# The two merge gates of a hybrid encoder's mixer: sixteen plain products per layer rewritten as eight pairs of seven block products

## The chip, the cores and the metric

The kernel runs on one core of one Trainium2 chip. The metric is the device time of that core in microseconds (us). The median of three runs of the kernel before is 1674.38 us (1673.81 to 1674.62). The core's engines are TensorE (PE, with its weight load listed apart as PEld), VectorE (DVE), ScalarE (ACT), GpSimd (POOL) and SyncE (SP), which issues most of the DMAs.

## What is computed

Two layers of an encoder on a sequence of 512 rows of width 1024, in float32. Each layer is a mixer (attention and a short convolution side by side, merged by two sigmoid gates) and a SwiGLU feed-forward part (FFN). Cut to what matters:

```python
for l in range(DEPTH):                       # DEPTH = 2
    h = rms_norm(x, g_pre_mix[l])
    q, k, v, cb, cc, cx, ga, gb = jnp.split(h @ w_in[l], splits, axis=-1)
    ...
    y_attn = band_attention(q, k, v, attn_sink[l]) @ w_attn_proj[l]
    y_conv = (cb * short_conv(cc * cx, conv_w[l])) @ w_conv_proj[l]
    mix = (jax.nn.sigmoid(ga) * y_attn + jax.nn.sigmoid(gb) * y_conv) @ w_out[l]
    x = x + rms_norm(mix, g_post_mix[l])
    h = rms_norm(x, g_pre_ffn[l])
    f = (jax.nn.silu(h @ w_gate[l]) * (h @ w_up[l])) @ w_down[l]
    x = x + rms_norm(f, g_post_ffn[l])
```

`ga` and `gb` are 1024 columns each of the input projection `h @ w_in`.

## The kernel before

**Precision.** Every float32 operand is held as a high part (rounded to the format that TensorE takes) and a low part (the rest), and every product is three matmuls: high by low, low by high, high by high (`mm3`, L175 to L177). Splitting a weight tile is one ACT copy that rounds (L130) and one DVE subtraction (L131), for a tile of 128 partitions by 512 elements; splitting an activation is the same pair on L206 and L207.

**Plain products.** `gemm` computes 128 output columns for all 512 rows of the sequence: 8 steps along the width, 3 matmuls each, 24 matmuls of 512 moving columns. Its weights come by one DMA of 512 KB into one of three `raw` tiles and are split into two of eight `hl` tiles.

**Seven block products.** The FFN's gate and up products are done in pairs (`class Pair`): for one block f, 128 columns of w_gate and 128 of w_up are the two rows of a 2 by 2 block matrix whose columns are the two halves of the width, and the activations are a 2 by 2 block matrix too (halves of the width by halves of the sequence). Seven products of sums of blocks replace the eight plain ones. Each product is 4 steps of 3 matmuls with 256 moving columns. `Pair.prep` adds weight blocks on DVE (L393) and splits each sum (L130, L131); `Pair.product` runs the matmuls and takes the results out of the banks with small ACT and DVE instructions (L434 to L448). Loads of the second matrix go into tiles of the pool `u4` (22 buffers). `orders` writes down in which order the products of several pairs follow each other, and weights are prepared `AHEAD = 5` products early. The sums of the activations' blocks (`Rights`) are made once per layer.

**The stage of the change.** After the attention and the convolution's projection (`conv_proj`), a loop over m = 0 to 7 runs three plain products: the columns `GB0 + m` of w_in, a sigmoid (L783) and a multiplication by the convolution's branch (L785); the columns `GA0 + m` and their sigmoid (L788); the attention's projection, a multiplication (L791), an addition (L792) and a split into `mix[m]`. Then `down` multiplies by w_out: rows k = 0 to 2 stream through `hl` tiles for all eight output banks, rows 3 to 7 are split into ten `u4` tiles and kept, and the last part runs row block by row block (t = 0 to 3), so that the normalisation of block t (`post_norm`, L257 to L264; `pre_norm`, L236) goes on beside the products of block t + 1. In between stand the loads and splits of the first FFN weights (`ahead`).

**Order.** A scheduler puts each engine's instructions into one fixed order when the program is built; each engine then runs its own list strictly in that order and waits where an operand or a buffer isn't there. The rows under the change below show these lists.

## Time and profile before

| | |
|---|---|
| median of three runs | 1674.38 us |
| the profiled execution: its time, its span | 1674.66 us, 1672.9 us |
| busy: PE, PEld, DVE, ACT, POOL | 1650.1, 1454.9, 1141.8, 862.7, 72.3 us |
| first layer: loop over m, from its first matmul to the first of `down` | 314.35 to 444.90 us |
| second layer: the same | 1141.06 to 1271.62 us |

Busy time is the sum of an engine's instruction spans; overlapping spans count once. A row of the timeline gives the start, the duration, the engine, the line and the operation, and in square brackets for how long the engine had been idle and what released it. Matmuls overlap in the pipeline, so their pace is read from the distance between starts.

### The profile page before, as it was taken

The page shows a single profiled execution, that of the slowest core. Times are in us where ns is not written, and L with a number is a line of the kernel's source. Part 1 is how long each engine was busy: PE and PEld are TensorE (multiplying, and loading weights), DVE is VectorE, ACT ScalarE, POOL GpSimd, SP SyncE. Part 2 cuts the span into 40 slices and gives each one's busy share as a digit, 9 for nine tenths or more (in the row PEclk, how much of TensorE's full clock was granted, in tenths as well). Part 3 has the DMA queues.
Part 4 walks back from the last instruction along what each step waited for, and adds up shares of the span by engine and source line. Part 5 has one row for each costly group of instructions (what it writes and reads, how often), then busy time and mean ns, then how long its engine had stood idle before and what let it go on. Part 6 is the DMA issues. An engine that isn't in the chain of part 4 may idle for free.

```text
span 1672.9 us, 24896 instructions
## 1 busy us (share of the span) xinstructions
PE 1650.1 (99%) x9457; PEld 1454.9 (87%) x9457; DVE 1141.8 (68%) x2230; ACT 862.7 (52%) x1806; POOL 72.3 (4%) x114
## 2 busy tenths in 40 slices
PE   7999999999999999999999999999999999999998
PEld 7888888888889999988898888888888899999886
DVE  6988876434469988854469788754434899888442
ACT  5566666433346655543346666564333555556331
POOL 0000000000011100000000000000000011001000
PEclk9999999999999999999999999999999999999999
DMA  6322222433452333343413222224335333434332
GB/s 201 94 76 76 65 87 64 133 95 101 129 161 76 102 102 101 115 138 127 150 64 101 76 76 76 76 76 126 101 100 164 101 92 99 108 103 133 111 115 76
DMA packets 246937, 174.35 MB, mean 104 GB/s; under 512 B 5488, under 2 KB 232864, under 8 KB 246816
## 3 DMA queue, kind: packets, MB, share of 16 engines
q1 hardware_dynamic: 246096, 171.18, 34.6%
q8 instruction: 74, 1.21, 0.3%
q10 hardware_dynamic: 720, 1.57, 0.3%
q14 instruction: 47, 0.39, 0.1%
HBM read 164.34 MB, written 8.39 MB: 103 GB/s over the span
## 4 chain that ended last, share of the span: by engine, by line
PE 97%; DVE 2%; ACT 1%; DMA 0%; POOL 0%; issue 0%; POOLq 0%; DVEq 0%; ACTq 0%
PE bank L176 30%; PE bank L177 30%; PE bank L175 30%; PE bank L627 2%; PE bank L674 2%; PE bank L661 2%; PE bank L244 0%; DVE u L207 0%; DVE h L207 0%; DMA t<-in_x_dram 0%; ACT t L228 0%; PE bank L327 0%; DVE t L264 0%; POOL r L222 0%; DVE t L236 0%
## 5 line engine op out<-in xcount | busy, mean ns | idle before, releaser
L175 PE MATMUL bank<-h,hl 128*128 128x256 f32 (+1 forms) x1536 | 521.6, 340 | 1.1 <-DVE h L207 1.1
L176 PE MATMUL bank<-h,hl 128*128 128x256 f32 (+1 forms) x1536 | 518.2, 337 | 0.0
L177 PE MATMUL bank<-h,hl 128*128 128x256 f32 (+1 forms) x1536 | 517.8, 337 | 0.0
L131 DVE TENSOR_TENSOR hl<-raw,hl 128x512 fp32r<-128x512 f32 x428 | 292.8, 693 | 230.9 <-ACT hl L130 228.3
L130 ACT CAST hl<-raw 128x512 fp32r<-128x512 f32 x428 | 261.6, 620 | 323.4 <-PE bank L177 241.5
L177 PEld LDWEIGHTS bank<-h,hl 128*128 128x128 f32 x1536 | 292.2, 190 | 30.9
L175 PEld LDWEIGHTS bank<-h,hl 128*128 128x128 f32 x1536 | 292.5, 190 | 29.3 <-DVE h L207 1.9
L176 PEld LDWEIGHTS bank<-h,hl 128*128 128x128 f32 x1536 | 292.5, 190 | 27.6
L175 PE MATMUL bank<-u,hl 128*128 128x256 f32 (+1 forms) x784 | 251.2, 321 | 3.4 <-DVE u L207 3.4
L176 PE MATMUL bank<-u,hl 128*128 128x256 f32 (+1 forms) x784 | 250.2, 319 | 2.7 <-ACT u L206 1.8
L177 PE MATMUL bank<-u,hl 128*128 128x256 f32 (+1 forms) x784 | 250.0, 319 | 0.0
L175 PEld LDWEIGHTS bank<-u,hl 128*128 128x128 f32 x784 | 149.7, 191 | 13.8 <-DVE u L207 3.8
L176 PEld LDWEIGHTS bank<-u,hl 128*128 128x128 f32 x784 | 149.9, 191 | 13.0 <-ACT u L206 2.2
L177 PEld LDWEIGHTS bank<-u,hl 128*128 128x128 f32 x784 | 150.0, 191 | 10.3
L130 ACT CAST hl<-t 128x512 fp32r<-128x512 f32 x176 | 108.3, 621 | 58.2 <-DVE t L393 41.1
L131 DVE TENSOR_TENSOR hl<-t,hl 128x512 fp32r<-128x512 f32 x176 | 133.4, 765 | 6.0 <-ACT hl L130 3.9
L175 PE MATMUL bank<-hl,u 128*128 128x512 f32 x304 | 118.3, 389 | 0.0
L176 PE MATMUL bank<-hl,u 128*128 128x512 f32 x304 | 118.3, 389 | 0.0
L177 PE MATMUL bank<-hl,u 128*128 128x512 f32 x304 | 118.3, 389 | 0.0
L647 ACT ACTIVATE t<-t,neg 128x256 f32<-128x256 f32 (+1 forms) x128 | 70.4, 552 | 21.1 <-DVE neg L642 20.8
L632 DVE CUSTOM_DVE_ANT_0 t<-bank,tab,sink 128x256 f32<-128x256 f32 (+1 forms) x128 | 65.7, 541 | 6.1 <-PE bank L627 5.9
L448 POOL TENSOR_TENSOR u<-t 128x256 f32<-128x256 f32 x44 | 51.9, 1179 | 397.4 <-DVE t L444 236.6
(123 smaller groups left out, 2121.4 us busy)
## 6 DMA issues: line engine op xcount, KB each, us to landing
raw<-in_w_in_dram SPq DMA_DIRECT2D x104, 512.0 KB, 3.9
u<-in_w_up_dram SPq DMA_DIRECT2D x44, 512.0 KB, 5.9
raw<-in_w_down_dram SPq DMA_DIRECT2D x44, 512.0 KB, 3.5
raw<-in_w_gate_dram SPq DMA_DIRECT2D x40, 512.0 KB, 4.0
raw<-in_w_conv_proj_dram SPq DMA_DIRECT2D x16, 512.0 KB, 4.2
raw<-in_w_attn_proj_dram SPq DMA_DIRECT2D x16, 512.0 KB, 4.3
raw<-in_w_out_dram SPq DMA_DIRECT2D x16, 512.0 KB, 3.5
xd<-t SPq DMA_DIRECT2D x12, 512.0 KB, 2.9
```

The lines of the kernel that those rows point to most:

```text
L130: nc.scalar.copy(h, raw)
L131: eng.tensor_tensor(out=lo, in0=raw, in1=h.bitcast(F32), op=ALU.subtract)
L175: nc.tensor.matmul(acc, wh, xl, start=first, stop=False, skip_group_check=goes_on)
L176: nc.tensor.matmul(acc, wl, xh, start=False, stop=False, skip_group_check=goes_on)
L177: nc.tensor.matmul(acc, wh, xh, start=False, stop=last, skip_group_check=goes_on)
L448: nc.gpsimd.tensor_tensor(out=out[:, TH:], in0=c22, in1=self.g[:, TH:], op=ALU.mult)
L627: nc.tensor.matmul(s[:, :w], q, kk[g][:, 1 - part, lo_b * P : lo_b * P + w], start=part == 0, stop=part == 1)
L632: nc.vector.tensor_tensor_reduce(out=p, in0=s[:, :w], in1=mask[:, m0 : m0 + w], scale=HD**-0.5, scalar=sink[:, h : h + 1], op0=ALU.add, op ...
L647: nc.scalar.activation(p, p, AF.Exp, bias=neg[:, i : i + 1], accum_out=den[:, i : i + 1])
L661: nc.tensor.transpose(pt[:, i * P : (i + 1) * P], p[:, n * P : (n + 1) * P], ident)
L674: nc.tensor.matmul(o, v, hl[:, 1 - part], start=n == 0 and part == 0, stop=kb == hi_b and part == 1)
```

## The change

The loop over m is taken apart. The attention's projection now runs first, eight plain products one after the other, and its results are kept (`ya`). Behind it the gate columns are done as eight pairs of seven block products, with the pair's two matrices taken from `GA0 + m` and `GB0 + m` of w_in. The block sums of the activations (`Mixed.sums`) are made from the activations that the layer already holds in `hT`; one product's operand is written back into `hT`'s place. `Pair` is made general: what is done with its two results stands in two methods, `first` and `second`, and the FFN's pairs (`Gated`) do there what `Pair` did before. `Gates.first` takes the sigmoid of the attention's gate and multiplies it by `ya`; `Gates.second` takes the sigmoid of the convolution's gate in two halves, multiplies by `yc`, adds, and splits into `mix[m]`. In each gate pair product 4 is split another way: ACT writes the high part (L135) and the negated rounded value into the low part's place (L136), and a DMA issued by GpSimd adds the unrounded source to it (L137). That step is issued up to ten products early. `orders` gets the number of pairs to begin with as an argument: 5 in the FFN as before, 2 for the gates.

```diff
+    def split_by_dma(h, lo, src):
+
+        nc.scalar.copy(h, src)
+        nc.scalar.activation(lo, src, AF.Copy, scale=-1.0)
+        nc.gpsimd.dma_start(out=lo.bitcast(F32), in_=src, accum_op=ALU.add)
+
...
+    class Mixed:
...
+            self.ops = {1: self.part[0, 0], 2: self.part[1, 0], 3: self.part[1, 1], 7: self.part[0, 1]}
...
+        def sums(self):
+            def whole(i, j):
+                h, lo = (x.bitcast(F32) for x in self.part[i, j])
+                x = t4([P, KH, TH])
+                nc.vector.tensor_tensor(out=x, in0=h, in1=lo, op=ALU.add)
+                return x
+
+            def put(p, x):
+                if p not in self.ops:
+                    self.ops[p] = tuple(unit([P, KH, TH]) for _ in range(2))
+                split_to(*self.ops[p], x)
+
+            x12 = whole(0, 1)
+            x11 = whole(0, 0)
+            nc.vector.tensor_tensor(out=x11, in0=x11, in1=x12, op=ALU.subtract)
+            put(5, x11)
+            x22 = whole(1, 1)
+            nc.vector.tensor_tensor(out=x12, in0=x22, in1=x12, op=ALU.subtract)
+            nc.vector.scalar_tensor_tensor(x22, x22, -1.0, x11, op0=ALU.mult, op1=ALU.subtract)
+            put(6, x22)
+            put(7, x12)
+            x21 = whole(1, 0)
+            nc.vector.scalar_tensor_tensor(x21, x22, -1.0, x21, op0=ALU.mult, op1=ALU.subtract)
+            put(4, x21)
...
             hl = hl_tile()
-            split_w(src, hl[:, 0], hl[:, 1])
+            if p in self.by_dma:
+                split_by_dma(hl[:, 0], hl[:, 1], src)
+            else:
+                split_w(src, hl[:, 0], hl[:, 1])
...
+    def run_pairs(pairs, seq, before=lambda n: None):
+        for n, (i, p) in enumerate(seq):
+            before(n)
+            for j, q in seq[n : n + 2 * AHEAD]:
+                pairs[j].need(q)
+                if q in pairs[j].by_dma:
+                    pairs[j].prep(q)
+            for j, q in seq[n : n + AHEAD]:
+                pairs[j].prep(q)
+            pairs[i].product(p)
...
-        mix = []
+        mix, ya = [None] * KT, [None] * KT
+        mixed = Mixed(hT)
+
+        class Gates(Pair):
+            by_dma = (4,)
+
+            def first(self):
+                nc.scalar.activation(self.out0, self.out0, AF.Sigmoid)
+                nc.vector.tensor_tensor(out=self.out0, in0=self.out0, in1=ya[self.m], op=ALU.mult)
+
+            def second(self):
+                m, out = self.m, self.out1
+                nc.scalar.activation(out[:, :TH], self.a, AF.Sigmoid, scale=-1.0)
+                nc.scalar.activation(out[:, TH:], out[:, TH:], AF.Sigmoid)
+                nc.vector.tensor_tensor(out=out, in0=out, in1=yc[m], op=ALU.mult)
+                nc.vector.tensor_tensor(out=out, in0=out, in1=self.out0, op=ALU.add)
+                u = unit([P, 2, T])
+                split_to(u[:, 0], u[:, 1], out)
+                mix[m] = u
+
+        gates = []
         for m in range(KT):
-            acc = gemm(w_in, GB0 + m * P, xs)
-            sg = t2([P, T])
-            nc.scalar.activation(sg, acc, AF.Sigmoid)
-            yb = t2([P, T])
-            nc.vector.tensor_tensor(out=yb, in0=sg, in1=yc[m], op=ALU.mult)
-            acc = gemm(w_in, GA0 + m * P, xs)
-            sg = t2([P, T])
-            nc.scalar.activation(sg, acc, AF.Sigmoid)
+            gates.append(Gates(mixed, w_in, GA0 + m * P, w_in, GB0 + m * P))
+            gates[m].m = m
+        mixed.sums()
+        for m in range(KT):
             acc = gemm(a["w_attn_proj"][l], m * P, lambda k, part: qs[k][:, part])
-            ya = t2([P, T])
-            nc.vector.tensor_tensor(out=ya, in0=acc, in1=sg, op=ALU.mult)
-            nc.vector.tensor_tensor(out=ya, in0=ya, in1=yb, op=ALU.add)
-            u = unit([P, 2, T])
-            split_to(u[:, 0], u[:, 1], ya)
-            mix.append(u)
+            if m % 2 == 0:
+                held["ya"] = t4([P, 2, T]) if m < KT // 2 else unit([P, 2, T], F32)
+            ya[m] = held["ya"][:, m % 2]
+            nc.scalar.copy(ya[m], acc)
+        run_pairs(gates, gate_seq)
```

The change moves instructions at three places of each layer. In the lists below, as in the profile, L is a line of the file that the list is of: the split of an activation is L207 before and L213 now, the last step of an attention unit L688 and L689 before and L751 and L752 now. The names are the program's, with buffer numbers.

**Place 1: DVE at the end of the attention, first layer.** `t4_76` is the split of the last attention weights, `t2_79` the last attention unit's result, `u4_16` and `u4_18` the tiles in which its split goes to the attention's projection. Before:

```order
L207 TENSOR_TENSOR t4_76_3138<-bank_173_3133,t4_76_3138 128x512
L131 TENSOR_TENSOR hl_93_3275<-raw_46_3270,hl_93_3275 128x512
L131 TENSOR_TENSOR hl_94_3311<-raw_47_3309,hl_94_3311 128x512
L688 TENSOR_TENSOR t2_79_3176<-bank_172_3130,t2_78_3175 64x256
L689 TENSOR_TENSOR t2_79_3176<-bank_172_3130,t2_78_3175 64x256
L207 TENSOR_TENSOR u4_16_1751<-t2_79_3176,u4_16_1751 128x128
L207 TENSOR_TENSOR u4_18_2058<-t2_79_3176,u4_18_2058 128x128
```

The same place now; L327, L337 and the L213 into `u4_27` belong to `Mixed.sums`:

```order
L327 TENSOR_TENSOR t4_77_3198<-h_0_86 128x1024
L213 TENSOR_TENSOR t4_76_3138<-bank_173_3133,t4_76_3138 128x512
L327 TENSOR_TENSOR t4_78_3200<-h_0_86 128x1024
L327 TENSOR_TENSOR t4_79_3207<-h_0_86 128x1024
L337 TENSOR_TENSOR t4_78_3200<-t4_78_3200,t4_77_3198 128x1024
L327 TENSOR_TENSOR t4_80_3217<-h_0_86 128x1024
L751 TENSOR_TENSOR t2_79_3176<-bank_172_3130,t2_78_3175 64x256
L752 TENSOR_TENSOR t2_79_3176<-bank_172_3130,t2_78_3175 64x256
L213 TENSOR_TENSOR u4_27_3204<-t4_78_3200,u4_26_3203 128x1024
L213 TENSOR_TENSOR u4_16_1751<-t2_79_3176,u4_16_1751 128x128
L213 TENSOR_TENSOR u4_18_2058<-t2_79_3176,u4_18_2058 128x128
```

Five instructions of 1024 elements now stand between the split of the attention weights and the last two splits for the projection, and a sixth stands ahead of them; the weight subtractions into `hl_93` and later moved behind.

**Place 2: ACT where the gate products begin, first layer.** `hl_110` to `hl_116` are weight tiles of the first two pairs, `bank_183` and `bank_184` their banks. The rows of the list now (before, ACT has plain weight splits and the sigmoids of L783 and L788 here):

```order
L130 CAST hl_110_3561<-t2_81_3521 128x512
L135 CAST hl_111_3577<-u4_34_3504 128x512
L136 ACTIVATE hl_111_3577<-u4_34_3504 128x512
L482 COPY t4_83_3545<-bank_183_3526 128x256
L130 CAST hl_112_3582<-t2_80_3520 128x512
L130 CAST hl_113_3603<-t2_83_3540 128x512
L130 CAST hl_114_3621<-t2_81_3521 128x512
L482 COPY t4_84_3585<-bank_184_3564 128x256
L135 CAST hl_115_3638<-u4_35_3506 128x512
L136 ACTIVATE hl_115_3638<-u4_35_3506 128x512
```

The tile of the first pair's product 4, `hl_111`, is filled between those of the seventh product in line (`hl_110`) and the eighth (`hl_112`), though product 4 of that pair is the thirteenth; the second pair's, `hl_115`, stands behind the copy of that pair's product 1. On POOL, eight DMAs (L137) per layer follow each other in its list with nothing between them.

**Place 3: SP at the end of the gate products, first layer.** Loads of the last gate weights (w_in), of w_out and of the first FFN weights. Before:

```order
L140 DMA raw_67_4047<-in_w_attn_proj_dram 128x8x128
L165 DMA raw_68_4099<-in_w_out_dram 128x1024
L165 DMA raw_69_4131<-in_w_out_dram 128x1024
L165 DMA raw_70_4163<-in_w_out_dram 128x1024
L165 DMA raw_71_4195<-in_w_out_dram 128x1024
L165 DMA raw_72_4203<-in_w_out_dram 128x1024
```

And now:

```order
L171 DMA raw_60_4585<-in_w_out_dram 128x1024
L417 DMA u4_44_4173<-in_w_in_dram 128x8x128
L417 DMA u4_46_4307<-in_w_in_dram 128x8x128
L171 DMA raw_61_4617<-in_w_out_dram 128x1024
L217 DMA t4_91_4573<-in_g_post_mix_dram 128x1024
L217 DMA t4_92_4575<-in_g_pre_ffn_dram 128x1024
L171 DMA raw_62_4649<-in_w_out_dram 128x1024
L884 DMA t4_93_4783<-in_x_dram 128x1024
L171 DMA raw_63_4681<-in_w_out_dram 128x1024
L171 DMA raw_64_4689<-in_w_out_dram 128x1024
```

The second matrices of the last two pairs (`u4_44`, `u4_46`) stand behind the first load of w_out, and the loads of the two gains and of x, which stood early in the loop over m before, stand among those of w_out.

## Rows read from the trace of the kernel before

**Rows 1.** The page: the span, the busy time of each engine (share, instructions), and the granted TensorE clock in tenths in 40 slices of the span.

```profile
span 1672.9 us, 24896 instructions
PE 1650.1 (99%) x9457; PEld 1454.9 (87%) x9457; DVE 1141.8 (68%) x2230; ACT 862.7 (52%) x1806; POOL 72.3 (4%) x114
...
PEclk9999999999999999999999999999999999999999
```

**Rows 2.** The waits of PE: line and tile, the engine and tile waited for, us in total, times, longest; the two left out are 1.8 and 0.9 us in total.

```profile
PE bank L244 <- DVE t L232: 9.4, 1, 9.4
PE bank L175 <- DVE u L207: 3.4, 2, 1.7
...
PE bank L175 <- DVE h L207: 1.1, 2, 0.5
```

**Rows 3.** The timeline of PE (start, duration): the first matmul of the loop over m, the first of the product behind it, the first of `down`, and the first of its kept part in the first layer; the first of the loop and of `down` in the second.

```profile
314.35 0.39 PE L175 MATMUL bank<-h,hl 128*128 128x512 f32 x1
...
319.79 0.39 PE L175 MATMUL bank<-h,hl 128*128 128x512 f32 x1
...
444.90 0.39 PE L175 MATMUL bank<-hl,u 128*128 128x512 f32 x1
...
461.22 0.39 PE L175 MATMUL bank<-u,u 128*128 128x512 f32 x1
...
1141.06 0.39 PE L175 MATMUL bank<-h,hl 128*128 128x512 f32 x1
...
1271.62 0.39 PE L175 MATMUL bank<-hl,u 128*128 128x512 f32 x1
```

**Rows 4.** The timeline of PE in the FFN of the first layer: the first matmuls of two block products that lie seven products apart.

```profile
600.38 0.28 PE L175 MATMUL bank<-h,hl 128*128 128x256 f32 x1
...
610.46 0.28 PE L175 MATMUL bank<-h,hl 128*128 128x256 f32 x1
```

**Rows 5.** Busy time by stretch: the loop over m of the first layer, and a stretch of its FFN in which only block products run; length, then busy us (instructions) of PE, PEld, DVE, ACT and POOL, the granted clock, the DMA share and GB/s.

```profile
314.35:444.90 130.55, 130.55 (x577) 108.11 (x576) 51.74 (x78) 43.31 (x74) 0.00 (x0) 1.00 0.33 100
560.00:700.00 140.00, 140.00 (x1169) 140.00 (x1169) 122.85 (x209) 79.86 (x154) 16.45 (x14) 1.00 0.39 105
```

**Rows 6.** The groups of instructions that price the added work: line, engine, operation, names, shapes, count, busy us in total, mean ns of one, idle time before.

```profile
L131 DVE TENSOR_TENSOR hl<-raw,hl 128x512 fp32r<-128x512 f32 x428 | 292.8, 693 | 230.9 <-ACT hl L130 228.3
L435 DVE TENSOR_TENSOR t<-bank,t 128x256 f32<-128x256 f32 x44 | 18.4, 418 | 8.4 <-ACT t L434 8.4
L236 DVE SCALAR_TENSOR_TENSOR t<-t,r,t 128x1024 f32<-128x1024 f32 x12 | 15.4, 1284 | 7.0 <-POOL r L222 7.0
L130 ACT CAST hl<-raw 128x512 fp32r<-128x512 f32 x428 | 261.6, 620 | 323.4 <-PE bank L177 241.5
L434 ACT COPY t<-bank 128x256 f32<-128x256 f32 x44 | 16.4, 374 | 33.7 <-PE bank L177 33.7
L228 ACT ACTIVATE t<-t 128x1024 bf16<-128x1024 f32 x16 | 16.9, 1058 | 26.4 <-DVE t L264 22.6 <-DMA t<-in_x_dram 3.8
```

**Rows 7.** The timeline of DVE in the FFN where it runs back to back: two neighbours of 512 elements, and one of 256 with its neighbour.

```profile
586.86 0.67 DVE L131 TENSOR_TENSOR hl<-raw,hl 128x512 fp32r<-128x512 f32 x1
587.46 0.68 DVE L393 TENSOR_TENSOR t<-raw,u 128x512 f32<-128x512 f32 x1
...
588.66 0.41 DVE L435 TENSOR_TENSOR t<-bank,t 128x256 f32<-128x256 f32 x1
589.00 0.67 DVE L131 TENSOR_TENSOR hl<-t,hl 128x512 fp32r<-128x512 f32 x1
```

**Rows 8.** The timeline of DVE at the end of the attention of the first layer (Place 1).

```profile
305.61 0.69 DVE L131 TENSOR_TENSOR hl<-raw,hl 128x512 fp32r<-128x512 f32 x1 [0.49 <-ACT hl L130]
307.83 0.69 DVE L207 TENSOR_TENSOR t<-bank,t 128x512 fp32r<-128x512 f32 x1 [1.53 <-ACT t L206]
...
313.26 0.43 DVE L688 TENSOR_TENSOR t<-bank,t 64x256 f32<-64x256 f32 x1 [0.58 <-ACT t L686]
...
314.48 0.49 DVE L207 TENSOR_TENSOR u<-t,u 128x128 fp32r<-128x128 f32 x2 [0.36 <-ACT u L206]
```

**Rows 9.** DMA issues: what, from which queue, how many, KB each, median us from issue to landing: the shortest, a common one and the longest of the table.

```profile
out_dram<-t ACTq DMA_DIRECT2D x4, 256.0 KB, 2.1
raw<-in_w_in_dram SPq DMA_DIRECT2D x104, 512.0 KB, 3.9
tab<-tab_dram SPq DMA_DIRECT2D x1, 704.0 KB, 7.6
```

**Rows 10.** The timeline of DVE in `down` of the first layer: the first six and the last two splits of kept weights, the last two splits of the first FFN weights, and two early steps of the normalisation of row block 0 (L257 needs the first half of its columns, L260 the second).

```profile
447.82 3.69 DVE L131 TENSOR_TENSOR u<-raw,u 128x512 fp32r<-128x512 f32 x6
...
455.83 1.29 DVE L131 TENSOR_TENSOR u<-raw,u 128x512 fp32r<-128x512 f32 x2 [1.24 <-ACT u L130]
...
463.05 1.29 DVE L131 TENSOR_TENSOR hl<-raw,hl 128x512 fp32r<-128x512 f32 x2 [2.32 <-ACT hl L130]
465.54 0.15 DVE L257 TENSOR_SCALAR v<-ss 128x1 f32<-128x1 f32 x1 [1.20 <-ACT t L228]
...
468.94 0.16 DVE L260 TENSOR_TENSOR v<-ss,v 128x1 f32<-128x1 f32 x1 [2.65 <-ACT t L228]
```

**Rows 11.** The timeline of POOL in the FFN: two instructions of one shape.

```profile
561.29 4.67 POOL L448 TENSOR_TENSOR u<-t 128x256 f32<-128x256 f32 x1 [8.26 <-DVE t L444]
570.91 0.74 POOL L448 TENSOR_TENSOR u<-t 128x256 f32<-128x256 f32 x1 [4.95 <-DVE t L444]
```

More of the change, by code (lines that the diff above doesn't have):

```diff
@@ L301, in encoder, with __init__, op @@
     KH = KT // 2
+    class Mixed:
+        def __init__(self, hT):
+            self.part = {
+                (i, j): tuple(hT[:, part, i * KH : i * KH + KH, j * TH : j * TH + TH] for part in range(2))
+                for i in range(2) for j in range(2)
+            }
+            self.ops = {1: self.part[0, 0], 2: self.part[1, 0], 3: self.part[1, 1], 7: self.part[0, 1]}
+        def op(self, p):
+            return self.ops[p]
+        def sums(self):
[20 more added lines that the diff above has]
+            put(4, x21)
     class Rights:
@@ L424, in product @@
                 self.v = t4([P, 4, TH])
[L425 removed]
+                self.out0, self.out1 = (self.v[:, i : i + 2].rearrange("p a t -> p (a t)") for i in (2, 0))
             acc = self.b if p == 2 else self.c if p in (5, 3) else self.a
@@ L464, in free @@
             return p == 1 or len(seq) - at[i, before] >= 3
-        for i in range(EARLY):
+        for i in range(early):
             seq += [(i, 2), (i, 1)]
@@ L812, in encoder, with first, second @@
         act = [None] * FT
-        wg, wu = a["w_gate"][l], a["w_up"][l]
-        pairs = [Pair(wg, wu, f * P, r) for f in range(FT)]
+        class Gated(Pair):
+            def first(self):
+                nc.scalar.activation(self.out0, self.out0, AF.Silu)
+            def second(self):
+                f = self.f
+                if f % 2 == 0:
+                    held["act"] = unit([P, 2, T], F32)
+                out = act[f] = held["act"][:, f % 2]
+                nc.vector.scalar_tensor_tensor(
+                    out[:, :TH], self.a, -1.0, self.out0[:, :TH], op0=ALU.mult, op1=ALU.mult
+                )
+                nc.gpsimd.tensor_tensor(out=out[:, TH:], in0=self.v[:, 1], in1=self.out0[:, TH:], op=ALU.mult)
+        pairs = []
+        for f in range(FT):
+            pairs.append(Gated(r, a["w_gate"][l], f * P, a["w_up"][l], f * P))
+            pairs[f].f = f
         def ahead():
@@ L827, in encoder, with turn_rest @@
         xsrc = dst
-        def gated(f):
-            if f % 2 == 0:
-                held["act"] = unit([P, 2, T], F32)
-            act[f] = held["act"][:, f % 2]
-            return act[f]
-        for f, pr in enumerate(pairs):
-            pr.dst = lambda f=f: gated(f)
-        for n, (i, p) in enumerate(seq):
+        def turn_rest(n):
             if n == 1:
@@ L846, in encoder @@
                 r.sums(3)
-            for j, q in seq[n : n + 2 * AHEAD]:
-                pairs[j].need(q)
-            for j, q in seq[n : n + AHEAD]:
-                pairs[j].prep(q)
-            pairs[i].product(p)
+        run_pairs(pairs, seq, turn_rest)
         last = l == DEPTH - 1
```

47 lines of the change are left out of this document (24 added, 23 removed).

## The prediction

> **What bounds the kernel now.** I read the page first: PE is busy for 1650.1 of 1672.9 us and the clock stands at its upper level, 2.4 GHz, in all 40 slices [rows 1]. Then the waits of PE: 9.4 us are the first load, and no other wait comes to more than 3.4 us in total [rows 2]. So TensorE bounds the program from end to end, and what a change is worth is what it takes out of PE's stream, less the waits that it puts in. In the loop over m PE never pauses, while DVE works 51.74 and ACT 43.31 of 130.55 us [rows 5]: there is room beside it for other engines' work. The FFN's block products are the model of what the gates become: PE without a pause there too, but DVE busy for 122.85 of 140 us [rows 5].
>
> **The change, part by part.** *PE.* The loop over m takes 444.90 - 314.35 = 130.55 us in the first layer and 130.56 in the second [rows 3]; that is 24 plain products of 319.79 - 314.35 = 5.44 us, 0.2267 us a matmul. Now eight plain products stay, 8 x 5.44 = 43.5 us. Sixteen become 56 block products. Seven of them take 610.46 - 600.38 = 10.08 us in the FFN [rows 4], 1.44 us each and 0.120 us a matmul, so 56 take 80.6 us. Together 124.2: 6.4 us less per layer, **12.8 us** for both. Moving columns fall by an eighth in those sixteen products, time by less, since 256 columns cost more than half of 512: in the FFN stretch the weight load is busy for all 140 us, in the loop over m for 108 of 130.55 [rows 5], so the narrow products run at the pace of the weight loads. The gate products have the same shape as the FFN's, and I take 0.120 us.
>
> The Trainium skill ("TensorE: Matmul & The Clock Gate", section "Back-to-back issue gap") gives 518 cycles for 512 columns and 262 for 256, which at 2.4 GHz is 0.216 and 0.109 us; by these the saving would be 384 x 0.2158 - 672 x 0.1092 = 9.5 us per layer and the time about 1655.4. The trace has 0.2267 and 0.120 for this kernel's float32 operands, and the measurement decides.
>
> *DVE during the gate products.* Per pair: four additions and six weight subtractions (product 4 has none), one multiplication in `first`, two instructions and a split in `second`, which is 14 instructions of 512 elements, and three of 256 that take results out of the banks. Back to back they cost 0.60 and 0.34 us (587.46 - 586.86, 589.00 - 588.66) [rows 7], so 14 x 0.60 + 3 x 0.34 = 9.42 us; standing alone 0.693 and 0.418 [rows 6], so 10.96 us. PE takes 10.08 us per pair. Which end? The same count for an FFN pair (11 and 4) gives 7.96 back to back, and the trace shows 122.85 / 140 x 10.08 = 8.85, a factor of 1.11; for the gates that is 10.47, and this is the value I take. DVE then loses 0.39 us per pair on PE, 3.1 us over eight pairs. The cover is the lead: when the last plain product runs it holds two of the eight `hl` tiles and six are ready for the gates, 6 x 1.44 = 8.6 us of PE's work. Even at 10.96 the loss is 7.0 us. So I charge nothing; with the cover gone, every 0.1 us per pair beyond would cost 0.8 us per layer.
>
> *ACT.* Per pair nine instructions of 512 at 0.62 us, five of 256 at 0.374 and one sigmoid of 512 at about 0.62 [rows 6]: 8.1 us against 10.08. Nothing.
>
> *The block sums.* Twelve DVE instructions of 1024 elements at 1.28 us (15.4 us) and four ACT casts at 1.06 [rows 6] per layer, beside the projection's 43.5 us, in which DVE otherwise has 16 weight subtractions (11.1 us). What matters is Place 1. DVE is free at 306.3; one sum takes it to 307.6, the attention's split comes at 307.83 as before, and four more sums take it from 308.5 to 313.6, where L688 came at 313.26 [rows 8]. Its two steps end at 314.5. The subtraction into `u4_27` waits for a cast of 1.06 us and ends near 315.8, and the last two splits near 316.3; before, they ended at 314.97. The projection, which now starts at 314.35 at once, needs those two tiles in its seventh and eighth of eight steps, 6 x 0.68 = 4.1 us in, at 318.4. Two us to spare: nothing.
>
> *The adding DMA.* Per pair it takes one subtraction off DVE and puts one instruction on ACT. No row shows an adding DMA or one issued by POOL. The nearest are a store of 256 KB, 2.1 us to landing, loads of 512 KB, 3.9, and the longest of the table, 7.6 [rows 9]; I take 4, nearest to the common load. POOL beside a busy DVE can stretch: one shape took 0.74 us and 4.67 us [rows 11], which would make it 8. Its deadline, by Place 2: the second pair's value is written behind the copy of that pair's product 1 (the fourth product, ended at 5.8 us of the gate stage), so by 7.4 us, and its product 4 is the sixteenth, at 21.6 us. That leaves 14.2 us; the first pair has 17.3 - 1.2 = 16.1. Eight DMAs stand in POOL's list with nothing behind them that is due before `down`. Hidden.
>
> *The end of the stage.* The first FFN weights and the kept rows of w_out, which were loaded and split beside idle engines, are now split after the gates. Let D be the start of `down`. The last product 4 runs behind ten matmuls of `down`, so it ends at D + 3.7, and its sigmoid, two multiplications and additions and the split (0.37 + 0.69 + 0.69 + 0.62 + 0.69) hold DVE to D + 6.8. From there the pace is that of loads through three `raw` tiles. Before, the kept splits took from 447.82 to 457.1 and those of the FFN to 464.34 [rows 10], 9.3 and 16.5 us, so now D + 16.1 and D + 23.3. The kept part of `down` needs its weights at D + 16.3 + 1.4 = D + 17.7. The normalisation's L257 stands behind these splits in DVE's list; it came 4.3 us after the kept part's start [rows 3, 10] and would now be due at D + 22.0, so it is 1.3 us late, but L260, which waits for the second half anyway at 7.7 us, D + 25.4, swallows that. The margins are 1.6 and some 1.2 us; the places of the loads of the gains and of x (Place 3) could eat them. I charge 0.4 us for both layers, and up to 3 us per layer as the bound.
>
> *Sum.* 1674.66 (the profiled execution: its span of 1672.9 and 1.8 around it) - 12.8 + 0.4 = 1662.3; it stood 0.3 above the median of the runs, so **1662.0 us**. A gain beyond 12.8 would have to come out of the few us of PE's other waits [rows 2]; I allow 2.
>
> **The rivals.** *DVE becomes the bound of the gate stage.* For: 93 to 109% of PE's time per pair, more than anywhere in the trace. Against: the lead of 8.6 us, and that a late DVE runs back to back. At 11.5 us per pair it costs 8 x 1.42 - 8.6 = 2.8 us per layer and gives 1667.6; at 11.95 the whole gain is gone, which needs 27% over back to back.
>
> *The end of the stage is late*, by 1 to 3 us per layer: 1664 to 1668.
>
> *PE waits for the adding DMA, and the kernel is slower.* The step that fails is product 4 of each pair, when the DMA takes over 14.2 us from issue to landing. Two pairs are in flight, so an excess y is paid once per two pairs, 4y per layer; at y = 1.6, a landing of 15.8 us, the gain is gone. If the whole DMA stretched like POOL's instruction (4.67 / 0.74, so 3.9 to 24.6 us) it were 4 x 10.4 = 42 us per layer: 1745. Against it: the rows next to it are 2.1 to 7.6 us, and no DMA of the table needs half of 14.2.
>
> The Trainium skill ("SBUF — State Buffer", section "SBUF: two separate sides") speaks against the change here: a DMA issued from GpSimd has its descriptors written by that engine, which a DVE instruction in a two-port mode locks out, and "Who interferes with whom" gives 620 ns that become 3100. A fivefold landing of 19.5 us would make 4 x 5.3 us per layer, 1704. The same section doubts that additions of two tensors do this, and DVE's instructions here are of that kind; no run here shows it yet. By the page "DMA: Bandwidth & Descriptors" (the anatomy of a DMA on the gpsimd path), 2.0 us and 256 KB at 436 GB/s would be an estimate of 2.6 us.
>
> *The narrow matmuls run faster than in the FFN*, at half of 0.2267: 672 x 0.0067 = 4.5 us per layer more, 1653. The FFN's rows speak against it.
>
> **How the numbers follow.** Forecast, 1659.5 to 1664: 0.70. DVE as the bound: 0.10, of which 0.03 lie at or above the time before. The end of the stage: 0.08. The adding DMA: 0.05, all slower. Narrow matmuls faster: 0.02. Something not seen here takes the gain: 0.05, half of it slower. A measurement of this kernel can tell 0.2%, 3.3 us, from no change, so faster means under 1671: 0.70 + 0.07 + 0.08 + 0.02 = 0.87; slower 0.05 + 0.015 + 0.025, about 0.08; the same 0.05. The range 1659.5 to 1668.5 holds the forecast, the milder DVE case and the late end, 0.85.
>
> **What would show it.** The stretch from the first projection product to the first matmul of `down` at 124.2 us in each layer; matmuls of the gates 0.120 us apart; no wait of PE on `hl` tiles of the gates, DVE at 90% or more there; the DMA of L137 landing in under 8 us; the last splits for the projection near 316.3; L257 within 2.5 us of its old place behind the kept part's start. I am wrong if PE waits in product 4, if DVE's lead melts before the eighth pair, or if the kept part of `down` starts late.

## The result and the profile after

The changed kernel took **1662.55 us** (median, 1662.28 to 1663.51) where the kernel before, measured beside it, took 1674.45: a ratio of 0.9931 with a 95% interval of 0.9913 to 0.9948, 11.9 us. The forecast was 1662.0. The profiled execution took 1662.62 us, with a span of 1660.8.

Line numbers below are those of the changed kernel or of the run named: the three matmuls are L181 to L183 (L175 to L177 before), the split of an activation ends on L213 (L207), and the two steps of the normalisation, L257 and L260 in [rows 10], are L263 and L266. L492 is the DVE instruction that empties a bank behind product 7.

The page: the span and the busy engines.

```profile
span 1660.8 us, 26449 instructions
...
PE 1636.2 (99%) x10033; PEld 1470.2 (89%) x10033; DVE 1237.5 (75%) x2398; ACT 929.5 (56%) x1958; POOL 86.2 (5%) x130
```

Against [rows 1] TensorE has 576 matmuls more and 13.9 us less to do, and DVE 95.7 us more. The clock is at its upper level in all 40 slices, as before. A queue that is new in the page's third part, with 4.20 MB, is that of the adding DMAs, 16 times 256 KB.

The timeline of PE: the first matmul of the projection, of the gates, of `down` and of its kept part in layer 1; the first transposed row block that the FFN reads; and the projection and `down` of layer 2. What stands in brackets is a wait.

```profile
314.06 0.39 PE L181 MATMUL bank<-u,hl 128*128 128x512 f32 x1
...
357.58 0.28 PE L181 MATMUL bank<-h,hl 128*128 128x256 f32 x1
...
436.77 0.40 PE L181 MATMUL bank<-hl,u 128*128 128x512 f32 x1
...
454.58 0.39 PE L181 MATMUL bank<-u,u 128*128 128x512 f32 x1
...
484.64 0.39 PE L181 MATMUL bank<-h,hl 128*128 128x256 f32 x1 [0.87 <-DVE h L213]
...
1134.68 0.39 PE L181 MATMUL bank<-u,hl 128*128 128x512 f32 x1
...
1257.39 0.40 PE L181 MATMUL bank<-hl,u 128*128 128x512 f32 x1
```

The stage takes 436.77 - 314.06 = 122.71 us, and one more product of 1.44 us, the last product 4, runs inside `down`: 124.15, in place of 130.55 [rows 3]. Layer 2 gives the same 122.71. So the two stages give back 12.8 us. The account closes: the first stage begins 0.29 us earlier than before (314.06 for 314.35); the wait at 484.64 is 0.33 us longer than its counterpart before; the FFN of layer 2 has one wait of 0.61 us, at 1498.57, that was not there. 12.8 + 0.3 - 0.3 - 0.6 is 12.2, and the spans differ by 12.1.

The waits of PE (line and tile, engine and tile waited for; us in total, times, longest; one of 0.2 us is left out). None of them lies in the gate products of either layer:

```profile
PE bank L250 <- DVE t L238: 9.5, 1, 9.5
PE bank L181 <- DVE u L213: 3.4, 2, 1.7
PE bank L182 <- ACT u L212: 1.8, 2, 0.9
PE bank L182 <- DVE hl L131: 1.5, 4, 0.5
PE bank L181 <- DVE h L213: 1.4, 2, 0.9
PE bank L181 <- DVE t L492: 0.6, 1, 0.6
```

Three short waits more than before, 0.72 us together, lie near 1330, at the start of the FFN of layer 2. They do not lengthen it: from the wait ahead of them to the next one behind them it is 12.23 us, and 12.24 before.

The stretch of the gate products in layer 1, as in [rows 5] (length, then busy us of PE, PEld, DVE, ACT and POOL, the clock, DMA share, GB/s):

```profile
357.58:436.50 78.92, 78.92 (x659) 78.92 (x658) 72.01 (x126) 58.90 (x119) 7.09 (x8) 1.00 0.54 138
```

TensorE does not pause; PEld, which was busy for 108 of 130 us in the old loop, is busy all the time, as in the FFN; DVE stands at 91%. The DVE timeline, first at the end of attention, where the last splits that the projection needs are to be seen, then around the end of the stage, as in [rows 10]:

```profile
314.05 1.63 DVE L213 TENSOR_TENSOR u<-t,u 128x1024 fp32r<-128x1024 f32 x3 [0.22 <-ACT u L212]
...
452.34 1.29 DVE L131 TENSOR_TENSOR u<-raw,u 128x512 fp32r<-128x512 f32 x2 [1.59 <-ACT u L130]
...
460.02 1.29 DVE L131 TENSOR_TENSOR hl<-raw,hl 128x512 fp32r<-128x512 f32 x2 [2.34 <-ACT hl L130]
461.23 0.15 DVE L263 TENSOR_SCALAR v<-ss 128x1 f32<-128x1 f32 x1
...
462.30 0.16 DVE L266 TENSOR_TENSOR v<-ss,v 128x1 f32<-128x1 f32 x1 [0.33 <-ACT t L234]
```

And line L137, the adding DMA: the time of its issue on POOL (least, median and largest, in ns) and of its landing.

```profile
L137 POOL DMA_DIRECT2D hl<-u x16: 852/860/1032, 360.8 to 1243.5; - x16
...
DMA to landing us min/median/max: 3.3/4.8/7.3
```

### The profile page after: what moved, and what is told of

Read it like the earlier page. It is cut to its first block, busy times and chain, and to the rows that moved or that the text cites. A ratio compares the mean times of both kernels' runs of the same rounds, so it can differ in the third digit from the quotient of the medians.

```text
span 1660.8 us, 26449 instructions
## 1 busy us (share of the span) xinstructions
PE 1636.2 (99%) x10033; PEld 1470.2 (89%) x10033; DVE 1237.5 (75%) x2398; ACT 929.5 (56%) x1958; POOL 86.2 (5%) x130
## 4 chain that ended last, share of the span: by engine, by line
PE 96%; DVE 2%; DMA 1%; ACT 1%; issue 0%; POOL 0%; POOLq 0%; DVEq 0%; SPq 0%; ACTq 0%
PE bank L182 30%; PE bank L183 29%; PE bank L181 29%; PE bank L690 2%; PE bank L737 2%; PE bank L724 2%; PE bank L250 0%; DVE u L213 0%; DMA u<-in_w_up_dram 0%; DVE h L213 0%; DMA t<-in_x_dram 0%; ACT t L234 0%; DVE t L438 0%; DVE hl L131 0%; PE bank L372 0%
## 5 line engine op out<-in xcount | busy, mean ns | idle before, releaser
L181 PE MATMUL bank<-h,hl 128*128 128x256 f32 (+1 forms) x1536 | 493.7, 321 | 1.4 <-DVE h L213 1.4
L182 PE MATMUL bank<-h,hl 128*128 128x256 f32 (+1 forms) x1536 | 490.4, 319 | 0.4 <-DVE hl L131 0.4
L183 PE MATMUL bank<-h,hl 128*128 128x256 f32 (+1 forms) x1536 | 490.1, 319 | 0.0
L131 DVE TENSOR_TENSOR hl<-raw,hl 128x512 fp32r<-128x512 f32 x396 | 269.9, 692 | 167.6 <-ACT hl L130 166.2
L130 ACT CAST hl<-raw 128x512 fp32r<-128x512 f32 x396 | 241.8, 620 | 258.8 <-PE bank L183 216.7
L183 PEld LDWEIGHTS bank<-h,hl 128*128 128x128 f32 x1536 | 292.7, 191 | 20.8
L181 PEld LDWEIGHTS bank<-h,hl 128*128 128x128 f32 x1536 | 292.9, 191 | 19.9 <-DVE h L213 2.2
L181 PE MATMUL bank<-u,hl 128*128 128x256 f32 (+1 forms) x976 | 305.6, 313 | 4.1 <-DVE u L213 3.4
L182 PE MATMUL bank<-u,hl 128*128 128x256 f32 (+1 forms) x976 | 304.7, 312 | 2.9 <-ACT u L212 1.8
L183 PE MATMUL bank<-u,hl 128*128 128x256 f32 (+1 forms) x976 | 304.1, 312 | 0.0
L181 PEld LDWEIGHTS bank<-u,hl 128*128 128x128 f32 x976 | 186.6, 191 | 15.3 <-DVE u L213 3.8
L182 PEld LDWEIGHTS bank<-u,hl 128*128 128x128 f32 x976 | 186.8, 191 | 13.4 <-ACT u L212 2.2
L183 PEld LDWEIGHTS bank<-u,hl 128*128 128x128 f32 x976 | 186.8, 191 | 10.2
L131 DVE TENSOR_TENSOR hl<-t,hl 128x512 fp32r<-128x512 f32 x240 | 176.9, 745 | 22.5 <-ACT hl L130 19.9
L130 ACT CAST hl<-t 128x512 fp32r<-128x512 f32 x240 | 147.6, 621 | 72.4 <-DVE t L438 47.0
L181 PE MATMUL bank<-hl,u 128*128 128x512 f32 x304 | 118.3, 389 | 0.0
L183 PE MATMUL bank<-hl,u 128*128 128x512 f32 x304 | 118.3, 389 | 0.0
L438 DVE TENSOR_TENSOR t<-t,raw 128x512 f32<-128x512 f32 x112 | 76.7, 696 | 1.2
```

What stands on the lines that cost most here:

```text
L130: nc.scalar.copy(h, raw)
L131: eng.tensor_tensor(out=lo, in0=raw, in1=h.bitcast(F32), op=ALU.subtract)
L181: nc.tensor.matmul(acc, wh, xl, start=first, stop=False, skip_group_check=goes_on)
L182: nc.tensor.matmul(acc, wl, xh, start=False, stop=False, skip_group_check=goes_on)
L183: nc.tensor.matmul(acc, wh, xh, start=False, stop=last, skip_group_check=goes_on)
L438: add = lambda out, x, y: nc.vector.tensor_tensor(out=out, in0=x, in1=y, op=ALU.add)
```

## The experiments

The theory: the gain is the pace of TensorE's block products alone, and everything that was put beside them is covered. The rivals are those of the prediction: DVE as the bound, the adding DMA as the bound, a late end of the stage; and that the new order brings the gain. All kernels are edits of the changed one. The runs were taken in several sessions, in which the median of the kernel before lay between 1674.12 and 1674.65 us, so differences of half a microsecond between rows say nothing. "Stretch" is the time from the first gate product to the kept part of `down`, read from PE's timeline: 454.58 - 357.58 = 97.00 us in the changed kernel, 97.00 in layer 2 too.

| kernel | median us | ratio to before, 95% interval | stretch, layers 1 and 2 |
|---|---|---|---|
| changed kernel | 1662.55 | 0.9931 (0.9913 to 0.9948) | 97.00, 97.00 |
| order_alone | 1674.64 | 1.0003 (0.9994 to 1.0012) | 103.36, 103.36 |
| halves | 1670.52 | 0.9977 (0.9968 to 0.9987) | 99.51, 97.01 |
| no_dma | 1663.65 | 0.9935 (0.9923 to 0.9948) | 97.02, 97.02 |
| late_end | 1663.47 | 0.9937 (0.9925 to 0.9950) | 97.00, 97.01 |
| dma_5_ahead | 1670.24 | 0.9976 (0.9966 to 0.9986) | 100.74, 99.60 |
| dma_3_ahead | 1681.86 | 1.0044 (1.0028 to 1.0060) | 106.89, 105.30 |
| dve_plus_3 | 1677.34 | 1.0018 (1.0008 to 1.0028) | 103.78, 103.79 |
| dve_plus_5 | 1690.47 | 1.0096 (1.0080 to 1.0112) | 111.20, 110.17 |
| loads_15_ahead | 1665.96 | 0.9951 (0.9938 to 0.9963) | 98.17, 97.78 |
| dve_plus_3_lead_6 | 1673.72 | 0.9995 (0.9986 to 1.0004) | 101.99, 101.99 |
| after_loads_15 | 1663.35 | 0.9934 (0.9921 to 0.9946) | 97.00, 97.00 |

**Is it the pace, or the order?** order_alone keeps the new order and makes the gates plain products again.

```diff
-        mixed.sums()
...
-        run_pairs(gates, gate_seq)
+        for m in range(KT):
+            acc = gemm(w_in, GB0 + m * P, xs)
...
+            nc.vector.tensor_tensor(out=sg, in0=sg, in1=ya[m], op=ALU.mult)
```

> Only the order of the changed kernel: the eight projection products first, then sixteen plain gate products of 512 columns, no block sums, no adding DMA. The theory that the gain comes from the pace of TensorE's block products alone expects the loop at 24 x 5.44 = 130.6 us again in each layer and the whole at 1674 to 1675 us, 12 us above the changed kernel. A rival, that part of the gain comes from the new order (the projection starts 0.3 us earlier, the loads stand elsewhere), expects 1671 or less.

1674.64 us: the time before, with 87.04 us for sixteen plain gate products, 16 x 5.44. The order brings nothing that can be told; the rival is out. Against its stretch of 103.36 us the block products take 6.36 less per layer.

halves prices a narrow matmul in another place, where no other work is added.

```diff
-            acc = gemm(a["w_attn_proj"][l], m * P, lambda k, part: qs[k][:, part])
+            acc = bank()
+            hl = w_cols(a["w_attn_proj"][l], m * P)
+            for h in range(2):
+                gemm_half([acc], [hl], lambda k, part: qs[k][:, part], h)
```

> The changed kernel with each of the eight projection products run as two halves of 256 columns, so 48 matmuls of 256 in place of 24 of 512. If a narrow matmul costs 0.120 us, as the gate products show, a product takes 5.76 in place of 5.44 us: 16 x 0.32 = 5.1 us more, 1667.7. If the width alone counted (half of 0.2267 us each) there would be no difference, 1662.6; by the issue-gap figures of the Trainium skill (TensorE: Matmul & The Clock Gate, section Back-to-back issue gap; 0.216 and 0.109 us, an estimate) it would be 16 x 48 x 0.109 - 16 x 24 x 0.216 = 0.8 us, 1663.3.

It took 1670.52 us, 8.0 more in place of 5.1. The price is right: PE's timeline has the first two of these products 5.75 us apart, 48 matmuls of 0.120.

```profile
313.92 0.28 PE L181 MATMUL bank<-u,hl 128*128 128x256 f32 x1
...
319.67 0.28 PE L181 MATMUL bank<-u,hl 128*128 128x256 f32 x1
```

In layer 2 the way from the first projection product to `down` is 125.27 us, 122.71 + 2.56, exactly eight times 0.32. In layer 1 it is 2.36 us longer still, and the first sign is a wait of 0.78 us at 416.05, for DVE, which empties a bank late. DVE's timeline has the reason, a load of a pair's second weight for which it had stood still before:

```profile
405.82 0.69 DVE L438 TENSOR_TENSOR t<-u 128x512 f32<-128x512 f32 x1 [2.52 <-DMA u<-in_w_in_dram]
```

The load was issued at 397.90 and landed some 7.9 us later; why so late is not shown. It is not what the edit is about; a second weight that lands late comes up again in the runs on the adding DMA.

**Is DVE the bound, and is the DMA needed?** no_dma gives product 4 back to DVE.

```diff
-            by_dma = (4,)
+            by_dma = ()
```

> The changed kernel without the adding DMA: the low part of product 4 is subtracted on DVE like the others, eight instructions more per layer at 0.60 us, 4.8 us of DVE. In the changed kernel DVE was busy for 72.01 of 78.92 us of the gate stage, so 6.9 us are free. The theory that DVE is covered there expects the time unchanged, 1662.6, within 1 us. The rival, that DVE is already the bound of the stage and the DMA is needed, expects 2 x 4.8 = 9.6 us more, 1672.

1663.65 us, 1.1 us more, no difference that can be told from the changed kernel. DVE is busy for 75.73 of the 79.19 us from the first gate product to `down`, 96%, and TensorE still does not wait once in the gates. The adding DMA was not needed for this gain.

dve_plus_3 and dve_plus_5 look for the point at which DVE does become the bound. They write some low parts twice.

```diff
-            by_dma = (4,)
+            by_dma, again = (4,), (6, 7, 3)
...
+            if p in self.again:
+                nc.vector.tensor_tensor(out=hl[:, 1], in0=src, in1=hl[:, 0].bitcast(F32), op=ALU.subtract)
```

> The changed kernel with the subtractions of products 6, 7 and 3 of each gate pair done twice: 1.8 us more of DVE per pair. The changed kernel shows 72.01 us of DVE in 78.92, 9.2 per pair, so 11.0 against TensorE's 10.08: DVE falls 7.4 us behind over eight pairs, less than the lead of 8.6 us. The theory that the lead covers it expects 0 to 1 us in the whole, 1663. A second theory, that what the lead covers is handed on to the end of the stage, where the splits of the kept rows have 0.8 us to spare, expects about 6 us per layer there: 1675.

> The same with five subtractions done twice (products 2, 1, 6, 7 and 3): 3.0 us more, 12.2 per pair, 17 us behind over eight pairs. The lead of 8.6 us taken off, TensorE waits 8.4 us per layer in the gate products: 1679 by the lead alone, and with the end of the stage late as well by up to 7.8 us per layer: 1695.

They took 1677.34 and 1690.47 us, 14.8 and 27.9 more. Three subtractions a pair, which by the lead of the prediction should have been hidden, cost the whole gain and more. Of the 6.8 us per layer 5.85 lie in the gates (85.04 us for 79.19) and 0.93 between `down` and its kept part (18.74 for 17.81); so the end of the stage is not where the price is paid, and the second theory of the expectation falls too. For five, the gates take 92.46 and 91.43 us, 13.3 and 12.2 more, where the lead alone gave 8.4. The largest entry among PE's waits in dve_plus_3, behind the first load, is new (L463 is the second subtraction; us in total, times, longest):

```profile
PE bank L182 <- DVE hl L463: 4.8, 6, 1.4
```

By the prediction's sums DVE falls 8 x (9.42 + 1.80 - 10.08) = 9.1 us behind with three and 18.7 with five. The gates lost 5.85, and 13.3 and 12.2 in the two layers: by these sums the cover was 3.3 us in the one and 5.4 to 6.5 in the other, not 8.6.

Part of the reason stands in the changed kernel's own timelines, of DVE and of ACT, around the first gate product (357.58):

```profile
353.48 0.69 DVE L131 TENSOR_TENSOR hl<-t,hl 128x512 fp32r<-128x512 f32 x1 [4.14 <-ACT hl L130]
...
358.92 0.69 DVE L131 TENSOR_TENSOR hl<-t,hl 128x512 fp32r<-128x512 f32 x1 [2.94 <-ACT hl L130]
```

```profile
357.78 0.59 ACT L872 COPY u<-bank 128x512 f32<-128x512 f32 x1 [4.33 <-PE bank L183]
358.26 1.14 ACT L130 CAST hl<-t 128x512 fp32r<-128x512 f32 x2
```

The split at 353.48 is the fifth of the gates, and the sixth comes at 358.92. So five products are ready when the gates start, not six, and DVE stands still for the first 1.34 us of the gates: an estimate of the cover from these lines is 5 x 1.44 - 1.34 = 5.9 us. The cast that DVE waits for stands in ACT's list behind L872, the copy of the last projection product, which TensorE has just ended. Five tiles of the gates and two of that product leave one of the eight `hl` tiles free, so here it is the order of ACT's list, and not the tiles, that holds DVE up.

dve_plus_3_lead_6 asks what bounds this cover: the order in which DVE's list is written, or the eight `hl` tiles.

```diff
-            for j, q in seq[n : n + AHEAD]:
+            for j, q in seq[n : n + AHEAD + len(pairs[0].by_dma)]:
```

> The kernel with three subtractions of each gate pair done twice (1677.3 us), and the gates' preparation called for six products ahead in place of five. If DVE's lead is bounded by the order in which its list is written (the split of product n + 4 stands behind the bank operation of product n - 1), one product more is 1.44 us more of cover per layer: 1677.3 - 2.9 = 1674.4. If it is bounded by the eight hl tiles, as the prediction had it, nothing changes: 1677.3.

1673.72 us, 3.6 less than dve_plus_3 with the same tiles and the same instructions: 0.86 per layer in the gates (84.18), and the 0.93 at the kept part (17.81 again). PE's first wait in the gates comes 43.8 us behind their start in place of 32.6. So the order of the lists is part of what bounds the lead, which the theory of the eight tiles did not allow. But 0.86 us is less than the 1.44 expected, and 4.99 of the 5.85 us stay. DVE's wait across the start of the gates is still there at its full length, since the casts still stand behind the copy:

```profile
359.23 1.29 DVE L131 TENSOR_TENSOR hl<-t,hl 128x512 fp32r<-128x512 f32 x2 [2.94 <-ACT hl L130]
```

No run puts casts ahead of that copy, and what bounds the rest of the lead is open.

**The adding DMA.** dma_5_ahead issues it as late as the other splits; dma_3_ahead later still.

```diff
-                if q in pairs[j].by_dma:
-                    pairs[j].prep(q)
-            for j, q in seq[n : n + AHEAD]:
-                pairs[j].prep(q)
+            for d, (j, q) in enumerate(seq[n : n + AHEAD]):
+                if d < 3 or q not in pairs[j].by_dma:
+                    pairs[j].prep(q)
```

(dma_5_ahead has only the first two lines taken out.)

> The changed kernel with the adding DMA of product 4 issued like the other splits, five products ahead in place of ten: a lead of 5 x 1.44 = 7.2 us. From the copy of the bank before it (0.37 us) two ACT copies (1.24 us) and the landing (median 4.8, largest 7.3 us) make 6.4 to 8.9. The deadline theory expects an excess of 0 to 1.7 us per pair, paid in each of 16 products 4: 1662.6 to 1690, most likely about 1666. A rival, that the landing is hidden because ACT runs far ahead of TensorE, expects no change.

> The same DMA issued three products ahead: a lead of 4.3 us against 6.4. By the deadline theory TensorE waits 2.1 us at each product 4. If each pair pays it is 16 x 2.1 = 34 us, 1696; if, as the prediction said, an excess is paid once per two pairs, 17 us, 1679. The rival (hidden in any case) expects 1662.6.

1670.24 and 1681.86 us. In the profile with five products TensorE waited for the adding DMA once, 0.51 us, and not sixteen times; most of the 7.7 us lie elsewhere. SP's timeline, of the changed kernel and then of dma_5_ahead, shows it (L417 `u` loads the second weight of a pair):

```profile
404.99 0.35 SPq L171 DMA_DIRECT2D raw<-in_w_out_dram  x1
405.39 1.05 SPq L417 DMA_DIRECT2D u<-in_w_in_dram  x2
```

```profile
406.02 0.35 SPq L171 DMA_DIRECT2D raw<-in_w_out_dram  x1
406.42 0.43 SPq L417 DMA_DIRECT2D u<-in_w_in_dram  x1
417.24 0.34 SPq L171 DMA_DIRECT2D raw<-in_w_out_dram  x1
417.62 0.43 SPq L417 DMA_DIRECT2D u<-in_w_in_dram  x1
```

The edit moved one load of the pairs' second weights behind a load of `w_out`, which waits for a `raw` tile; it was issued 11 us later, at 417.62, and DVE stood still for 2.51 us until it landed:

```profile
425.73 0.69 DVE L438 TENSOR_TENSOR t<-u 128x512 f32<-128x512 f32 x1 [2.51 <-DMA u<-in_w_in_dram]
```

With three products TensorE waited for the DMA twice, once in each layer, 5.18 and 5.10 us; the other fourteen had landed in time. So neither "each pair pays" nor "once per two pairs" is right, and that 1681.86 lies near the 1679 of the second is luck. Two more of PE's waits in layer 1 (1.17 and 0.59 us) and one in layer 2 (0.60) are for banks that DVE emptied late; in layer 1 it had stood for 4.11 us until a second weight landed, which was issued behind a load of `w_out` here too. The POOL and SP timelines of dma_3_ahead, with the issue of the DMA that was late and what was issued around it:

```profile
430.50 0.86 POOL L137 DMA_DIRECT2D hl<-u  x1 [13.82 <-DVE t L856]
```

```profile
429.76 0.33 SPq L171 DMA_DIRECT2D raw<-in_w_out_dram  x1
430.14 0.42 SPq L217 DMA_DIRECT2D t<-in_g_post_mix_dram  x1
430.62 0.42 SPq L217 DMA_DIRECT2D t<-in_g_pre_ffn_dram  x1
431.14 0.38 SPq L883 DMA_DIRECT2D t<-in_x_dram  x1
```

Four loads of 512 KB go out within 1.4 us of each other beside it, and TensorE goes on at 440.34, 9.8 us after the issue; the longest landing of this run is 10.1 us, its median 5.7. In layer 2 it is the same, with the issue at 1260.34 among the same four loads and TensorE going on at 1270.10. That these loads make the landing long is read from the times; no run moves them alone.

loads_15_ahead leaves the late DMA of dma_5_ahead and calls for the weights earlier; after_loads_15 does only the latter to the changed kernel.

```diff
-            for j, q in seq[n : n + 2 * AHEAD]:
+            for j, q in seq[n : n + (3 if pairs[0].by_dma else 2) * AHEAD]:
```

> The kernel with the adding DMA five products ahead (1670.2 us), and the loads of the gate weights called for fifteen products ahead in place of ten. In that kernel DVE waited 4.9 us in the first gate stage for the second weights of pairs, since a load of w_out that waits for a raw tile had come to stand ahead of one of them in SP's queue; TensorE waited for the adding DMA itself only once, 0.5 us. The theory that the order of the loads makes its 7.6 us expects them mostly gone: 1663 to 1665. The rival, that the short lead of the adding DMA makes them, expects 1670 as there.

> The changed kernel with the loads of the gate weights called for fifteen products ahead and the rest as it is. In its profile neither TensorE nor DVE waits for a load in the gate stage of layer 1, so the theory that TensorE's stream sets the time expects no difference: 1662.6. A rival, that late loads cost something in the runs that the profile does not show, expects a gain of up to 1 us.

1665.96 and 1663.35 us. The second is the changed kernel's time: nothing to gain there. The first takes back 4.3 of the 7.7 us, more than half, so the late loads are the larger part of what the short lead cost; the stretches fall from 100.74 and 99.60 to 98.17 and 97.78, and what is left in them are waits for the adding DMA, 0.90 and 0.52 us. But its runs spread from 1664.26 to 1668.77 and the profiled one is the fastest of them, so where the slower ones lose 2 us more is open.

**The end of the stage.** late_end puts six more subtractions of DVE behind the splits of the kept rows.

```diff
             for i, p in seq[: 2 * READY]:
+                pairs[i].again = (p,)
                 pairs[i].prep(p)
+                pairs[i].again = ()
```

> The changed kernel with the six first FFN subtractions behind the kept rows done twice (the same values written again): 3.6 us more of DVE at the start of the kept part of down, so that L263 comes at about 464.8 in place of 461.23 and L266, due at 462.30, is 2.6 us late in each layer. The theory that each later block of rows (6.9 us of TensorE, some 5.4 us of chain) takes back 1.5 us expects nothing or up to 0.5 us in the whole: 1662.6 to 1663.1. The rival, that the end of the stage is on the path as soon as L266 is late, expects 2 x 2.6 = 5.2 us, 1667.8.

1663.47 us, 0.9 more, between the theories, and the profiled execution, the slowest of the runs (a span of 1664.1), shows both of them. In layer 1 most of the added work fell into DVE's waits for the casts of these splits (3.8 us of them behind the kept splits in the changed kernel, 1.05 left here), so that L266 was only 0.4 us late against the kept part's start, and the next row block had it back. In layer 2, DVE's timeline has L266 of the first and the third row block at the following times, here and then in the changed kernel:

```profile
1285.07 0.15 DVE L266 TENSOR_TENSOR v<-ss,v 128x1 f32<-128x1 f32 x1
...
1298.39 0.15 DVE L266 TENSOR_TENSOR v<-ss,v 128x1 f32<-128x1 f32 x1
```

```profile
1283.11 0.15 DVE L266 TENSOR_TENSOR v<-ss,v 128x1 f32<-128x1 f32 x1
...
1297.44 0.16 DVE L266 TENSOR_TENSOR v<-ss,v 128x1 f32<-128x1 f32 x1 [0.29 <-ACT t L234]
```

Behind the kept part's start (1274.51) these are 10.56 and 23.88 us, where the changed kernel (1275.20) has 7.91 and 22.24: 2.65 and 1.64 late, and 2.01 for the second block, at 1291.10. A row block takes back 0.4 to 0.6 us, not 1.5, and TensorE waits 2.16 us at the first block product of the FFN where it waited 0.53. What follows in the windows (columns as above) makes it dearer still:

```profile
1303.70:1305.86 2.16, 0.00 (x2) 0.00 (x1) 2.16 (x7) 1.20 (x4) 0.00 (x0) 1.00 0.00 0
1305.86:1311.00 5.14, 5.14 (x30) 5.14 (x31) 3.17 (x5) 1.21 (x2) 0.55 (x1) 0.67 0.43 120
```

After the pause the granted clock is 0.67 on the mean of 5.14 us, and the way to the next common wait takes 1.56 us more than in the changed kernel. That the end of the stage is on the path once the normalisation is late by more than the row blocks take back, is shown by layer 2 of this one, slowest execution; that it stays off the path in the changed kernel, by its own profile, where L266 comes in time.

## Why the prediction was right, point by point

- **TensorE, 6.4 us per layer.** Right: 124.15 for 124.2. halves and order_alone show that it is the pace of 0.120 us, and not the order. By an estimate from the 262 cycles of the Trainium skill ("TensorE: Matmul & The Clock Gate", section "Back-to-back issue gap") a projection product in halves would take 48 x 0.109 = 5.2 us; the trace shows 5.75. Why a narrow matmul costs 0.120 us is not shown. The prediction takes it for the pace of the weight loads, which are busy all the time; but 0.2267 - 0.120 = 0.107 us for 256 columns more is one column per cycle at 2.4 GHz, so 0.013 us that each matmul costs whatever its width would explain both values as well (an estimate).
- **DVE per pair, 10.47 us, and its cover.** The conclusion was right, both numbers were off. DVE took 72.01 / 78.92 x 10.08 = 9.2 us per pair, near the 9.42 back to back (the splits of the first five products lie ahead of this window, the end of the last pair behind it). The cover is not "six are ready for the gates, 6 x 1.44 = 8.6 us": that step failed. Five were ready, DVE stood still into the gates behind ACT's copy, and by the two tests the cover was worth 3 to 6 us. In this kernel the error cost nothing, since DVE did not need a cover; in that the forecast was lucky. The threshold of 11.95 us per pair was too high: at 9.42 + 1.80 = 11.2 the whole gain had gone.
- **The block sums.** The last of the three splits ended at 315.7, predicted 316.3; the projection needed them at 318.1. Nothing was paid.
- **The adding DMA.** Taken at 4 us, landed in 4.8 (3.3 to 7.3); hidden behind its deadline of 14.2 us, as said. The step "an excess is paid once per two pairs" is wrong: with the lead cut to three products two DMAs in sixteen were late. And the DMA is not needed: without it no difference in time can be told.
- **POOL beside a busy DVE.** The 16 issues took 852 to 1032 ns with DVE at 91%, and the DMAs landed in 3.3 to 7.3 us, not in the 19.5 of the rival. The fivefold time of the lock-out of which the Trainium skill ("SBUF — State Buffer", section "SBUF: two separate sides") warns does not show beside these DVE instructions, as that page itself held likely. (Its 620 and 3100 ns stand in the part on the bandwidth pool, beside a copy on DVE, and not under "Who interferes with whom".) A smaller stretch is not ruled out: no run has this DMA beside an idle DVE.
- **The end of the stage.** With D = 436.77: the first kept split at D + 7.1 (443.89; predicted 6.8), the kept splits done at D + 16.9 (predicted 16.1; needed at D + 17.8), the FFN's at D + 24.5 (predicted 23.3), L263 6.65 us behind the kept part's start, 2.3 later than before in place of 1.3. L266 came 7.72 us behind it, as before [rows 10]: swallowed. The margin was smaller than worked out, and late_end shows in layer 2 what it costs when it is used up.
- **The rest.** The charge was 0.4 us; measured, the waits outside the stages took 0.94 and the earlier start gave 0.29, so 0.65. The 0.61 us in the FFN of layer 2 come from a load of `w_up` that landed late (DVE stood for it 2.64 us, 1.88 at the same place before); that the change causes this is not shown.

## What to carry to other kernels

Where TensorE bounds a stage, a cut in its stream is worth its full price as long as each helper has its work ready; price the narrow matmul at what the trace shows for its width, not at its share of the columns. A helper's lead can be bounded by the order of the lists, its own and that of the engine it waits for, while a buffer is still free: count in the trace how many products are ready when the stage starts, see what the next one stands behind, and test the lead by adding work to that engine. An edit that moves a DMA or a split can move a load in a queue as well: compare the queues before a loss is put down to the edit's own transfer.

## What the runs showed of the hardware that was not expected

A pause of TensorE can cost more than itself. In layer 2 of dma_3_ahead it stood for 5.10 us behind the gates; the windows of a stretch before, of the pause and of what followed read (columns as above):

```profile
1250.00:1260.00 10.00, 10.00 (x86) 10.00 (x85) 7.21 (x13) 4.89 (x12) 0.00 (x0) 1.00 0.42 116
1265.00:1270.10 5.10, 0.00 (x1) 0.00 (x1) 1.54 (x3) 1.58 (x5) 0.00 (x0) 0.79 1.07 286
1270.10:1274.70 4.60, 4.60 (x21) 4.60 (x22) 1.43 (x3) 0.89 (x2) 0.00 (x0) 0.50 0.59 213
```

After the pause the clock stood at 0.50 for 4.6 us, the lower level of 1.2 GHz, and a matmul of 256 columns took 0.213 in place of 0.120 us: 21 of them, some 2.0 us on top of the 5.1. After the pause of 2.16 us in late_end it was 1.56 us on top. After shorter waits the clock fell in some places only: 0.87 us at 484.64 in the changed kernel and 1.37 us at 435.69 in dve_plus_3 left the clock at 1.00, while 1.18 us at 405.76 in dve_plus_5, close behind others, was followed by 4.2 us at 0.63.

An adding DMA of 256 KB from SBUF to SBUF took 3.3 us from issue to landing at best and 4.8 at the median in the changed kernel, where a common load of twice its size takes 3.9 [rows 9], and about 10 us in dma_3_ahead when four loads were issued with it.
